# Inverse square roots of three LayerNorm steps: three Newton steps from a bit pattern, or ScalarE's square root and one Newton step

## The chip, the core and the metric

The kernel runs on one core of one Trainium2 chip. The metric is the device time of one execution in microseconds (us); smaller is better. TensorE is called PE, VectorE DVE, ScalarE ACT, GpSimdE POOL; SP is the engine that issues most DMAs.

## The reference

One layer of a hybrid decoder on 512 tokens of 1024 features, in float32:

```python
h = layer_norm(x, ln_in_g, ln_in_b)
mix = hybrid_mixer(h, ...)            # 16 state-space heads and 8 latent-attention heads
h = layer_norm(ALPHA * h + mix, ln_mix_g, ln_mix_b)
ffn = peer(h, ...)                    # 8 heads pick 16 of 16384 experts for each token
h = layer_norm(ALPHA * h + ffn, ln_ffn_g, ln_ffn_b)

def layer_norm(x, g, b):
    mu = mean(x);  var = mean((x - mu) ** 2)
    return (x - mu) * rsqrt(var + 1e-5) * g + b
```

Each LayerNorm needs, for each token, the inverse square root of a variance plus 1e-5. This study is about how that one number per token is found at two places: in the first LayerNorm, and in the last one for the third block of 128 tokens.

## The kernel before, in words

The 512 tokens are four blocks of 128, with tokens on the partitions. The kernel is one long function that issues the instructions of each engine in the order in which they stand in the text: nothing reorders them, and each engine works through its own queue. A wait on one engine therefore holds up all that is behind it on that engine.

Weights come through one stream, `win` (class `Stream`): SP loads an item of 128x1024 into a raw buffer `wir` (L91), ACT rounds it to the high part `wih` (L109, method `his`), DVE forms the low part `wil` as the difference (L119, method `splits`), and a raw buffer is loaded anew once `splits` has used it. A product in float32 is three matmuls: high by high (L72), low by high (L73), high by low (L74).

**The first LayerNorm (L260 to L296).** SP first issues the four loads of x into `XH` (L248), then constants and the first three weight items. The four blocks are treated as two halves, p = 0 and p = 1. For each half DVE takes the statistics of two blocks (L268, L269), adds 1e-5 (L272), and calls `rsqrt` (L130 to L139) on a tile of 128x2: a shift and a subtraction on the bit pattern give a first guess (L133, L134), and three Newton steps of three operations each refine it (L136 to L138). `nm` is minus the mean times that root (L274). Then the blocks are normalised in place: both of the first half on ACT (L279); of the second half one block and half of the other on DVE (L281) and the remaining 512 columns on ACT (L279). PE transposes each block in eight pieces into eight PSUM tiles (L284). After the first half's transposes the text calls `win.his(2)`, so ACT rounds two weight items ahead of its part of the second half.

Then, for each of eight pieces k, ACT applies the gain and the bias (`ht`, L291), ACT or DVE writes the rounded `HH` (L293, L295), DVE the low part `HL` (L296). Ahead of this loop stands the first `splits`, behind its first piece the second. PE starts the first two products of the input projection from these.

**The middle.** The input projection with the state-space part, attention, output projection, the second LayerNorm, the expert scores, and a long stage over the 128 groups of 128 experts. Tokens of the last block are handled by gathers and end early; the other three blocks end in the PSUM tiles `va`.

**The tail (L1470 to L1504).** `ln_out(b)` finishes blocks 0, 1 and 2 in this order on DVE: add the residual (L1480, or L1478 for block 2), statistics (L1482, L1484), the inverse root, two wide products per half row (L1499 or L1492, and L1501), and the output DMAs (L1502; SP issues them, and ACT the last). The inverse root comes from the generator `norm_chain` (L141 to L157): the same bit pattern guess (L147, L149) and three Newton steps of two operations each (L152, L154). For block 2 the two products that don't need the root (L1492) are set between its steps. ACT has one operation ahead of this part, the scaling of block 2's residual (L1504), and then nothing but the last output issue.

Of the kernel before, what the change touches and what calls it, by code (L numbers as in the profile page):

```python
# [11 lines left out]
F32 = mybir.dt.float32  # L12
# [5 lines left out]
AF = mybir.ActivationFunctionType  # L18
OP = mybir.AluOpType
# [7 lines left out]
EPS = 1e-5  # L27
# [26 lines left out]
def tile_block(ctx: ExitStack, tc: tile.TileContext, I, out):  # L54
# [74 lines left out]
    def rsqrt(p, v, shape, tag):  # L129
# [8 lines left out]
            V.scalar_tensor_tensor(y, b, 1.5, y, op0=OP.add, op1=OP.mult)  # L138
        return y  # L139

    def norm_chain(p, mv, tag, out):  # L141
        v = [p.tile([128, 1], F32, name=tag + n, bufs=2) for n in "vhay"]
        ve, hv, a, y = v
        V.tensor_scalar(ve, mv[:, 1:2], EPS, None, op0=OP.add)
        V.tensor_scalar(hv, mv[:, 1:2], EPS, -0.5, op0=OP.add, op1=OP.mult)
        yield
        V.tensor_scalar(a.bitcast(U32), ve.bitcast(U32), 1, None, op0=OP.logical_shift_right)  # L147
        yield
        V.tensor_scalar(y.bitcast(U32), a.bitcast(U32), -1.0, float(0x5F3759DF), op0=OP.mult, op1=OP.add)  # L149
        for _ in range(3):  # L150
            yield
            V.scalar_tensor_tensor(a, y, hv, y, op0=OP.mult, op1=OP.mult)  # L152
            yield
            V.scalar_tensor_tensor(y, a, 1.5, y, op0=OP.add, op1=OP.mult)  # L154
        out.append(y)
        yield
# [10 lines left out]
    def norm_stats(p, t, tag):  # L167
# [4 lines left out]
            pass  # L172
        return mv, o[0]

    cs2 = pool("cs2", side="right")
    C = cs2.tile([128, C_END], F32, name="C")
    PAR = cs2.tile([128, P_END], F32, name="PAR")
# [80 lines left out]
    nc.sync.dma_start(idb, I["cb"][:, 640:768])  # L258

    V.memset(ones, 1.0)  # L260
    mv4 = lnp.tile([128, NB, 2], F32, name="mv4")
    PS8 = [pa() if k < 4 else pb() for k in range(8)]
    for p in range(2):
        bs = slice(2 * p, 2 * p + 2)
        for b in (2 * p, 2 * p + 1):
            st6 = lnp.tile([128, 2, 6], F32, name="st6", bufs=2)
            for i in range(2):
                V.bn_stats(st6[:, i], XH[:, b, i * 512:(i + 1) * 512])  # L268
            V.bn_aggr(mv4[:, b], st6.rearrange("p a b -> p (a b)"))  # L269
        ve = lnp.tile([128, 2], F32, name="ve", bufs=2)  # L270
        nm = lnp.tile([128, 2], F32, name="nm", bufs=2)
        V.tensor_scalar(ve, mv4[:, bs, 1], EPS, None, op0=OP.add)  # L272
        rs = rsqrt(lnp, ve, [128, 2], "l0")
        V.scalar_tensor_tensor(nm, mv4[:, bs, 0], -1.0, rs, op0=OP.mult, op1=OP.mult)  # L274
        for j, cs, act in (((0, slice(0, D), 1), (1, slice(0, D), 1)) if p == 0 else
                           ((0, slice(0, D), 0), (1, slice(0, 512), 1), (1, slice(512, D), 0))):
            t = XH[:, 2 * p + j, cs]
            if act:
                A.activation(t, t, AF.Identity, bias=nm[:, j:j + 1], scale=rs[:, j:j + 1])  # L279
            else:  # L280
                V.tensor_scalar(t, t, rs[:, j:j + 1], nm[:, j:j + 1], op0=OP.mult, op1=OP.add)  # L281
        for k in range(8):
            for b in (2 * p, 2 * p + 1):
                T.transpose(PS8[k][:, b * 128:(b + 1) * 128], XH[:, b, k * 128:(k + 1) * 128], ident)  # L284
        if p == 0:
            win.his(2)
    win.splits(1)
    for k in range(8):
        ht = lnp.tile([128, S], F32, name="ht", bufs=3)
# [1141 lines left out]
    fin = None  # L1431
# [39 lines left out]
    def ln_out(b):  # L1471
        t = xr[b]
        st = fin.tile([128, 2, 6], F32, name="fst", bufs=2)
        mv = fin.tile([128, 2], F32, name="fmv", bufs=2)
        ce = [slice(e * 512, (e + 1) * 512) for e in range(2)]
        for e in range(2):
            if b == 2:
                V.scalar_tensor_tensor(t[:, ce[e]], va[b][e], scl, t[:, ce[e]], op0=OP.mult, op1=OP.add)  # L1478
            else:
                V.scalar_tensor_tensor(t[:, ce[e]], t[:, ce[e]], ALPHA, va[b][e], op0=OP.mult, op1=OP.add)  # L1480
            yield
            V.bn_stats(st[:, e], t[:, ce[e]])  # L1482
            yield
        V.bn_aggr(mv, st.rearrange("p a b -> p (a b)"))  # L1484
        yield
        o = []
        ch = norm_chain(fin, mv, "lf", o)
        for i, _ in enumerate(ch):
            yield
            if b == 2 and i in (2, 4):  # L1490
                cs = ce[i // 2 - 1]
                V.scalar_tensor_tensor(t[:, cs], t[:, cs], mv[:, 0:1], R2[:, 0, cs], op0=OP.subtract, op1=OP.mult)  # L1492
                yield
        rs = o[0]
        for e in range(2):
            cs = ce[e]
            if b < 2:
                yield
                V.scalar_tensor_tensor(t[:, cs], t[:, cs], mv[:, 0:1], R2[:, 0, cs], op0=OP.subtract, op1=OP.mult)  # L1499
            yield  # L1500
            V.scalar_tensor_tensor(t[:, cs], t[:, cs], rs, R2[:, 1, cs], op0=OP.mult, op1=OP.add)  # L1501
            (nc.scalar if b == 2 and e else nc.sync).dma_start(out[b * 128:(b + 1) * 128, cs], t[:, cs])  # L1502

    A.activation(xr[2], xr[2], AF.Copy, scale=ALPHA)  # L1504
    kept = sorted(held)
    for b, cc in ((0, kept[:4]), (1, kept[:2]), (0, kept[4:]), (1, kept[2:])):
        for c in cc:
# [91 lines left out]
```

## Time and profile before

| what | value |
| --- | --- |
| median of 3 runs | 1627.26 us (1627.14 to 1628.96) |
| the profiled execution, its own time | 1627.28 us |
| its span, first to last instruction | 1625.5 us |
| PE busy | 1582.6 us, 97% of the span |
| DVE busy | 1377.3 us, 85% |
| ACT busy | 699.8 us, 43% |
| DMA | 393.77 MB, mean 242 GB/s |

The profile is that of one execution. A row of its timeline reads: start in us, time taken in us, engine, line, operation, what is written and read, and in brackets how long the engine sat idle before and what released it. PEld is PE's loading of the stationary operand; SPq and ACTq are the issues of DMAs. The chain of work that ended last is followed back from the last instruction; a list of waits gives total, number and longest; a row of stretches gives busy time of each engine, with the clock that PE was granted behind them.

### The profile page before, as it was taken

How to read it: one execution, taken by the hardware profiler on the slowest of the kernel's cores; microseconds unless marked ns; L12 is line 12 of the kernel's file. 1: busy time of each engine (PE TensorE's matmuls, PEld its weight loads, DVE VectorE, ACT ScalarE, POOL GpSimd, SP SyncE). 2: the span in 40 equal slices, each digit the busy share in tenths (PEclk: the TensorE clock that was granted, in tenths of full speed). 3: DMA queues.
4: the chain of work that ended last, by engine and by line, in shares of the span. 5: the costliest groups of instructions: out<-in, count | busy, mean ns of one | idle time of the engine just before them, and what ended most of it. 6: DMA issues, size and time to landing. Idle time of an engine off the chain costs nothing.

```text
span 1625.5 us, 23770 instructions
## 1 busy us (share of the span) xinstructions
PE 1582.6 (97%) x8640; PEld 1394.3 (86%) x8640; DVE 1377.3 (85%) x2649; ACT 699.8 (43%) x1213; POOL 463.3 (29%) x332
## 2 busy tenths in 40 slices
PE   7999999999999999999899999999999999999997
PEld 5777878888888999998899999999999999888886
DVE  8979688947799999999588788788888888988977
ACT  5575466641433545555433333343333333333341
POOL 0000000000143213200155455555554544533300
PEclk9999999999999999999999999999999999999999
DMA  6242121374432458766799999999999999999973
GB/s 245 91 157 91 46 64 47 103 242 143 135 92 86 123 182 292 285 240 244 251 375 345 339 331 354 344 338 343 329 355 337 344 329 352 360 335 342 335 220 122
DMA packets 150604, 393.77 MB, mean 242 GB/s; under 512 B 12536, under 2 KB 64584, under 8 KB 148696
## 3 DMA queue, kind: packets, MB, share of 16 engines
q1 hardware_dynamic: 107400, 237.76, 43.3%
q0 software_dynamic: 42944, 154.24, 26.2%
q8 instruction: 67, 1.10, 0.3%
q14 instruction: 49, 0.40, 0.1%
q10 hardware_dynamic: 144, 0.26, 0.0%
HBM read 359.66 MB, written 31.51 MB: 241 GB/s over the span
## 4 chain that ended last, share of the span: by engine, by line
PE 74%; DVE 21%; ACT 2%; issue 2%; DMA 1%; DVEq 0%; ACTq 0%; SPq 0%
PE va L1352 10%; PE va L1356 10%; PE va L1353 10%; PE pu L72 8%; PE pu L74 8%; PE pu L73 8%; PE pa L74 3%; PE pa L73 3%; PE pa L72 3%; DVE wil L119 3%; DVE ij L1109 3%; DVE g L1113 2%; DVE t L953 1%; PE pw L73 1%; PE pw L74 1%
## 5 line engine op out<-in xcount | busy, mean ns | idle before, releaser
L109 ACT ACTIVATE wih<-wir 128x1024 fp32r<-128x1024 f32 (+2 forms) x269 | 277.9, 1034 | 264.5 <-DMA wir<-v 90.5
L119 DVE TENSOR_TENSOR wil<-wir,wih 128x1024 fp32r<-128x1024 f32 (+1 forms) x254 | 302.2, 1190 | 103.2 <-ACT wih L109 43.0
L74 PE MATMUL pu<-XTH,wil 128*128 128x368 f32 x1008 | 331.9, 329 | 0.7 <-DVE wil L119 0.7
L72 PE MATMUL pu<-XTH,wih 128*128 128x368 f32 x904 | 299.3, 331 | 0.0
L73 PE MATMUL pu<-XTL,wih 128*128 128x368 f32 x904 | 297.0, 329 | 0.0
L1353 PE MATMUL va<-wil,Ph 128*128 128x512 f32 x726 | 282.7, 389 | 0.0
L1389 POOL DMA_INDIRECT row<-u,ix x128 | 187.6, 1465 | 230.1 <-DVE row L1400 136.7
L1389 POOL DMA_INDIRECT row<-v,ix x128 | 181.3, 1416 | 196.0 <-DVE ac L1406 167.6
L74 PEld LDWEIGHTS pu<-XTH,wil 128*128 128x128 f32 x1008 | 189.3, 188 | 1.3 <-DVE wil L119 1.3
L73 PEld LDWEIGHTS pu<-XTL,wih 128*128 128x128 f32 x904 | 170.0, 188 | 2.9
L72 PEld LDWEIGHTS pu<-XTH,wih 128*128 128x128 f32 x904 | 169.8, 188 | 2.9
L1352 PE MATMUL va<-wih,Ph 128*128 128x512 f32 x432 | 168.5, 390 | 0.0
L1406 DVE SCALAR_TENSOR_TENSOR ac<-row,hd,ac 128x1024 f32<-128x1024 f32 x128 | 164.0, 1281 | 3.0 <-DMA row<-v,ix 0.9
L1353 PEld LDWEIGHTS va<-wil,Ph 128*128 128x128 f32 x726 | 136.3, 188 | 25.9
L1205 ACT ACTIVATE act<-pu 128x368 f32<-128x368 f32 x126 | 59.9, 476 | 221.3 <-PE pu L74 196.3
L1400 DVE SCALAR_TENSOR_TENSOR row<-row,x 128x1024 f32<-128x1024 f32 x128 | 150.1, 1219 | 2.4 <-DMA row<-u,ix 2.4
L109 ACT ACTIVATE wihx<-wir 128x1024 fp32r<-128x1024 f32 x67 | 71.1, 1061 | 158.3 <-DMA wir<-v 129.9
L1356 PE MATMUL va<-wih,Pl 128*128 128x512 f32 x432 | 133.4, 390 | 0.0
L119 DVE TENSOR_TENSOR wil<-wir,wihx 128x1024 fp32r<-128x1024 f32 x62 | 75.9, 1223 | 51.4 <-issue 45.5
L1352 PE MATMUL va<-wihx,Ph 128*128 128x512 f32 x294 | 114.9, 391 | 0.9 <-ACT Ph L1336 0.9
L1356 PEld LDWEIGHTS va<-wih,Pl 128*128 128x128 f32 x432 | 81.1, 188 | 17.2
L1352 PEld LDWEIGHTS va<-wih,Ph 128*128 128x128 f32 x432 | 81.2, 188 | 15.8
(458 smaller groups left out, 3073.7 us busy)
## 6 DMA issues: line engine op xcount, KB each, us to landing
wir<-ut SPq DMA_DIRECT2D x128, 512.0 KB
wir<-v SPq DMA_DIRECT2D x128, 512.0 KB
gsp<-stg SPq DMA_DIRECT2D x12, 1920.0 KB
gt<-gsp SPq DMA_DIRECT2D x30, 768.0 KB
wir<-wo SPq DMA_DIRECT2D x26, 512.0 KB
wir<-wf SPq DMA_DIRECT2D x18, 512.0 KB
wir<-wqr SPq DMA_DIRECT2D x16, 512.0 KB
de<-acd POOLq DMA_DIRECT2D x8, 512.0 KB
```

The source lines that it names most:

```text
L72: T.matmul(ps, lh, rh, start=start, stop=False)
L73: T.matmul(ps, lh, rl, start=False, stop=False)
L74: T.matmul(ps, ll, rh, start=False, stop=stop)
L109: A.activation(h, r, AF.Copy)
L119: self.lo(n).tensor_tensor(l, r, h, op=OP.subtract)
L1205: A.activation(ACT[c][:, :NU], ps, AF.Gelu)
L1352: T.matmul(va[b][e], Ph[:, bs], h[:, cs], start=c == 0, stop=False)
L1353: T.matmul(va[b][e], Ph[:, bs], l[:, cs], start=False, stop=False)
L1356: T.matmul(va[b][e], Pl[:, bs], h[:, cs], start=False, stop=c == 127)
L1389: G.indirect_dma_start(out=R[s], out_offset=None, in_=I["u"] if s < 128 else I["v"], in_offset=bass.IndirectOffsetOnAxis(ap=ix[:, s % 128: ...
L1400: V.scalar_tensor_tensor(r, r, 1.0, x3, op0=OP.mult, op1=OP.mult, accum_out=hd[:, s:s + 1])
L1406: V.scalar_tensor_tensor(ac, r, hd[:, s - 128:s - 127], ac, op0=OP.mult, op1=OP.add)
```

## The change

A new function `sqrt_rs` takes the place of `rsqrt` in both halves of the first LayerNorm: ACT takes the square root of the variance with 1e-5 as its bias operand, while DVE forms -0.5 times the sum; then DVE takes the reciprocal and does one Newton step in three operations. The separate addition of 1e-5 (L272) is gone. A generator `sqrt_chain` does the same for block 2 of the tail, with a Newton step of two operations, and the two wide products now stand behind its first and its second step. A tile `eps` holds the constant. Two operations on a scrap tile `w0` take a square root on ACT ahead of need, one at the very start and one behind the scaling of block 2's residual. Last, one of the two weight roundings that ACT did behind the first half now stands ahead of ACT's part of the second half, behind the second square root, and the other behind that part.

```diff
+    def sqrt_rs(p, v, shape, tag):
+        h, q, y, a = (p.tile(shape, F32, name=tag + n) for n in "hqya")
+        A.activation(q, v, AF.Sqrt, bias=eps)
+        V.tensor_scalar(h, v, EPS, -0.5, op0=OP.add, op1=OP.mult)
+        V.reciprocal(y, q)
+        V.tensor_tensor(a, y, y, op=OP.mult)
+        V.tensor_tensor(a, a, h, op=OP.mult)
+        V.scalar_tensor_tensor(y, a, 1.5, y, op0=OP.add, op1=OP.mult)
+        return y
+
+    def sqrt_chain(p, mv, tag, out):
+        h, q, a, y = (p.tile([128, 1], F32, name=tag + n) for n in "hqay")
+        A.activation(q, mv[:, 1:2], AF.Sqrt, bias=eps)
+        V.tensor_scalar(h, mv[:, 1:2], EPS, -0.5, op0=OP.add, op1=OP.mult)
+        yield
+        V.reciprocal(y, q)
+        yield
+        V.scalar_tensor_tensor(a, y, h, y, op0=OP.mult, op1=OP.mult)
+        yield
+        V.scalar_tensor_tensor(y, a, 1.5, y, op0=OP.add, op1=OP.mult)
+        out.append(y)
+        yield
...
     V.memset(ones, 1.0)
+    V.memset(eps, EPS)
     mv4 = lnp.tile([128, NB, 2], F32, name="mv4")
+    w0 = lnp.tile([128, 1], F32, name="w0")
+    A.activation(w0, ones[:, 0:1], AF.Sqrt, bias=eps)
...
-        ve = lnp.tile([128, 2], F32, name="ve", bufs=2)
         nm = lnp.tile([128, 2], F32, name="nm", bufs=2)
-        V.tensor_scalar(ve, mv4[:, bs, 1], EPS, None, op0=OP.add)
-        rs = rsqrt(lnp, ve, [128, 2], "l0")
+        rs = sqrt_rs(lnp, mv4[:, bs, 1], [128, 2], f"l{p}")
         V.scalar_tensor_tensor(nm, mv4[:, bs, 0], -1.0, rs, op0=OP.mult, op1=OP.mult)
+        if p:
+            win.his(1)
...
-        if p == 0:
-            win.his(2)
+    win.his(2)
     win.splits(1)
...
-        ch = norm_chain(fin, mv, "lf", o)
+        ch = (sqrt_chain if b == 2 else norm_chain)(fin, mv, "ls" if b == 2 else "lf", o)
         for i, _ in enumerate(ch):
             yield
-            if b == 2 and i in (2, 4):
-                cs = ce[i // 2 - 1]
+            if b == 2 and i in (0, 1):
+                cs = ce[i]
...
     A.activation(xr[2], xr[2], AF.Copy, scale=ALPHA)
+    w0 = fin.tile([128, 1], F32, name="w0")
+    A.activation(w0, xr[2][:, 0:1], AF.Square)
+    A.activation(w0, w0, AF.Sqrt, bias=eps)
```

More of the change, by code (lines that the diff above doesn't have):

```diff
@@ L173, in norm_stats @@
         return mv, o[0]
+    ep = pool("ep", side="right")
+    eps = ep.tile([128, 1], F32, name="eps")
     cs2 = pool("cs2", side="right")
```

## The prediction

> **What bounds the kernel now.** I read the page first: who owns the chain that ended last, and what TensorE (PE) waited for.
>
> ```profile
> PE 74%; DVE 21%; ACT 2%; issue 2%; DMA 1%; DVEq 0%; ACTq 0%; SPq 0%
> ```
> ```profile
> PE pa L284 <- ACT XH L279: 11.6, 2, 10.9
> ```
>
> The first line is the chain by engine: PE owns 74% of the span, VectorE (DVE) 21%. The second opens the list of PE's waits (total, times, longest, in us): its longest, 10.9 us, is the wait for the first normalised block, at the very start. No wait of that list names a transfer. So whatever advances PE's start should be carried through the middle, where each stage is released by the one before it, and whatever is cut behind the last matmul is saved outright. The change works at these two ends, so I read the timeline of each.
>
> ```profile
> 6.81 0.21 DVE L269 BATCH_NORM_AGGREGATE mv<-st 128x2 f32<-128x12 f32 x1
> 7.05 0.17 DVE L272 TENSOR_SCALAR ve<-mv 128x2 f32<-128x2 f32 x1
> ...
> 7.87 0.33 SPq L254 DMA_DIRECT2D HR<-hrow  x1
> ...
> 9.21 0.33 SPq L91 DMA_DIRECT2D wir<-wf  x1
> ...
> 9.42 0.16 DVE L274 SCALAR_TENSOR_TENSOR nm<-mv,l0y 128x2 f32<-128x2 f32 x1
> ...
> 9.62 2.37 ACT L279 ACTIVATE XH<-XH,nm,l0y 128x1024 f32<-128x1024 f32 x2 [4.19 <-DVE nm L274]
> ...
> 10.89 0.33 SPq L258 DMA_DIRECT2D idb<-cb  x1
> ...
> 11.89 1.99 ACT L109 ACTIVATE wih<-wir 128x1024 fp32r<-128x1024 f32 x2
> ...
> 12.20 0.21 DVE L269 BATCH_NORM_AGGREGATE mv<-st 128x2 f32<-128x12 f32 x1
> ...
> 13.38 1.72 PEld L284 LDWEIGHTS pb<-ident,XH 128*128 128x128 f32 x8
> ...
> 14.82 0.16 DVE L274 SCALAR_TENSOR_TENSOR nm<-mv,l0y 128x2 f32<-128x2 f32 x1
> 15.02 0.81 ACT L279 ACTIVATE XH<-XH,nm,l0y 128x512 f32<-128x512 f32 x1 [1.14 <-DVE nm L274]
> ...
> 15.88 0.86 PEld L284 LDWEIGHTS pa<-ident,XH 128*128 128x128 f32 x8 [0.79 <-DVE XH L281]
> ...
> 16.20 1.22 DVE L119 TENSOR_TENSOR wil<-wir,wih 128x1024 fp32r<-128x1024 f32 x1
> 16.36 1.45 ACT L291 ACTIVATE ht<-pa,PAR 128x512 f32<-128x512 f32 x2 [0.54 <-PE pa L284]
> ...
> 17.34 0.42 DVE L295 CAST HH<-ht 128x512 fp32r<-128x512 f32 x1
> ...
> 20.27 0.19 PEld L73 LDWEIGHTS pa<-HL,wih 128*128 128x128 f32 x1 [0.30 <-DVE HL L296]
> ```
>
> From the aggregate (6.81) to nm (9.42) DVE walks twelve tiny dependent operations, about 0.195 us apart after a first step of 0.24, while ScalarE (ACT) idles 4.19 us. The same walk, 12.20 to 14.82, delays the second half. After 20.27 PE has no wait left in this stage: that is the moment I follow.
>
> **The change, step by step.** New is a 128x2 square root on ACT with a bias operand. The nearest groups (mean ns of one behind the comma):
>
> ```profile
> L456 ACT ACTIVATE de<-de,nac 128x128 f32<-128x128 f32 x64 | 19.6, 390 | 2.7 <-DVE de L461 2.7
> ...
> L279 ACT ACT_TABLE_LOAD x1 | 1.3, 1283 | 4.1 <-DMA XH<-x 4.1
> ...
> L1402 ACT ACTIVATE hd<-hd 128x128 f32<-128x128 f32 x1 | 0.3, 310 | 2.9 <-DVE row L1400 2.9
> ...
> L1057 ACT ACTIVATE uhd<-uhd 128x16 f32<-128x16 f32 x1 | 0.2, 218 | 0.0
> ```
>
> A 128x128 with a bias operand takes 0.39, without one 0.31; a 128x16 without one 0.22. I take 0.22 + 0.08 = 0.30, between bounds of 0.22 and 0.39. ACT followed nm by 0.20 (9.42 to 9.62), as a dependent DVE step would, so I give the way over the 0.24 and the way back 0.03. The reciprocal I price as any small DVE step.
>
> *First half.* Aggregate 6.81, square root 7.05 to 7.35, reciprocal 7.38, then four steps of 0.195 to nm: 8.16 in place of 9.42, **1.26 earlier**. DVE's half product (L144 of the changed kernel) runs beside the square root. The first table load (1.28) waits for x today; it moves ahead of that wait, with a warm-up root on a constant, under the time in which x is still loading: nothing. The 128x1 memset hides there too. DVE now reaches the third and fourth block of x 1.26 earlier, near 8.24 and 9.7. SP's HR issue (7.87) and third weight issue (9.21) waited, by the profile, for just these landings, so the data is there, by 0.4 us or more.
>
> *Second half.* Aggregate 12.20 - 1.26 = 10.94. ACT is done with the first two blocks at 9.62 + 2.37 - 1.26 = 10.73, so the second root isn't delayed; nm comes at 10.94 + 1.35 = 12.29 in place of 14.82, **2.53 earlier**. Of the two weight roundings that ACT did before this half (11.89, two in 1.99) only one now stands between, 11.5 to 12.5, and its weights had landed by 10.89, when idb's issue stopped waiting for them; it may end 0.01 or so after ACT would start normalising at 12.49. The other follows, 13.3 to 14.3.
>
> *PE's transposes.* The first half's last eight take 1.72 (0.215 each) from 13.38 and end at 15.10; moved by 1.26, at 13.84. The second half, which waited for XH until 15.88, is ready by then (12.49 + 0.81) and starts at 13.84, 2.0 earlier. In the run before it ran twice as fast (eight in 0.86): PE's pace doubled between 15.10 and 15.88. If it doubles at the same clock time, some eight go slowly and eight fast, to 13.84 + 1.72 + 0.86 = 16.4.
>
> *ht, HH, HL and the weights' low parts.* ht followed the transposes by 0.48; at the slow pace 0.2 more, so 14.5. HH follows 0.8 later at 15.3 in place of 17.34, where it waited for wil's end (16.20 + 1.22 = 17.42); that end is now 2.53 earlier and no longer last. HL, second wil and the 20.27 mark follow HH: 2.0 earlier. PE needs seven matmuls first, 0.23 each: 16.4 + 1.6 = 18.0, in time for 18.3. If the slow pace lasted through all 16 transposes, PE would arrive at 18.9, 1.4 earlier. If it rose early, wil binds: 2.5. I take **1.9**, range 1.2 to 2.5. Weight loads are issued when wil frees their buffers and move forward with it.
>
> *The middle.* In the changed program PE's and SP's orders are as before, and DVE's and ACT's differ only at the two ends; I cost it at nothing and carry 1.9 through.
>
> *The tail.* The last block:
>
> ```profile
> 1596.12 1.04 ACT L1504 ACTIVATE xr<-xr 128x1024 f32<-128x1024 f32 x1
> ```
> ```profile
> 1617.68 0.15 DVE L144 TENSOR_SCALAR lfv<-fmv 128x1 f32<-128x1 f32 x1
> ...
> 1618.06 0.15 DVE L149 TENSOR_SCALAR lfy<-lfa 128x1 uint32<-128x1 uint32 x1
> 1618.13 0.74 DVE L1492 SCALAR_TENSOR_TENSOR xr<-xr,fmv,R 128x512 f32<-128x512 f32 x1
> 1618.79 0.21 DVE L152 SCALAR_TENSOR_TENSOR lfa<-lfy,lfh 128x1 f32<-128x1 f32 x1
> 1619.03 0.16 DVE L154 SCALAR_TENSOR_TENSOR lfy<-lfa,lfy 128x1 f32<-128x1 f32 x1
> ...
> 1620.47 0.16 DVE L154 SCALAR_TENSOR_TENSOR lfy<-lfa,lfy 128x1 f32<-128x1 f32 x1
> 1620.66 1.41 DVE L1501 SCALAR_TENSOR_TENSOR xr<-xr,lfy,R 128x512 f32<-128x512 f32 x2
> 1622.16 0.37 ACTq L1502 DMA_DIRECT2D out_dram<-xr  x1
> ```
>
> New order: h at 1617.68; first wide product 0.07 later (as 1618.06 to 1618.13), 1617.75; reciprocal 0.66 on, 1618.41; second wide product 0.07 on, 1618.48; a 0.66 on, 1619.14; y 0.24 on, 1619.38; L1501 0.19 on, 1619.57 in place of 1620.66: **1.09 earlier**. ACT's root runs 1617.69 to 1618.0, covered by the first wide product with 0.4 to spare; uncovered it would cost at most its 0.3. Its table load is the only one added to the program: behind L1504 (ends 1597.2), before ACT's next work at 1622.16, so 1.28 in some 20 us of idleness. The output issue stays behind the root on ACT's queue; the root is done 3 us earlier.
>
> *Sum.* Profiled execution: span 1625.5, time 1627.28, 1.8 around it, 0.02 above the median 1627.26. 1627.28 - 1.9 - 1.09 = **1624.3**.
>
> **The rivals.** PE's clock by stretches (columns: length, busy PE, PEld, DVE, ACT, POOL, then the granted clock), and the chain behind:
>
> ```profile
> 222.13:225.54 3.41, 1.90 (x13) 1.34 (x11) 2.84 (x9) 2.00 (x6) 0.00 (x0) 1.00 0.00 0
> 223.64:227.05 3.41, 1.35 (x5) 0.63 (x4) 2.83 (x9) 3.23 (x9) 0.00 (x0) 1.00 0.00 0
> ...
> 227.05:230.46 3.41, 3.41 (x10) 2.64 (x9) 2.83 (x6) 0.48 (x1) 0.00 (x0) 0.50 0.33 96
> 261.19:264.60 3.41, 2.00 (x13) 1.37 (x11) 3.30 (x10) 2.37 (x6) 0.00 (x0) 1.00 0.43 124
> 264.60:268.01 3.41, 2.29 (x14) 1.76 (x14) 3.10 (x11) 2.23 (x6) 0.00 (x0) 1.00 0.02 5
> ```
> ```profile
> 227.24 0.43 PE pu L72
> ...
> 230.63 0.23 PE pu L74
> ```
>
> A stretch in which PE was busy 1.35 of 3.41 us is followed by one at half clock, in which eight matmuls of the chain take 0.43, not 0.23: 1.6 us. A stretch with 2.00 busy (261.19) is not followed by one.
>
> *(a) The half-clock stretch goes.* If the 3.41 us marks stand at the same times after the start, work that comes 1.9 earlier puts into the stretch before 223.64 what now lies in 222.13 to 225.54: 1.90 busy, nearer to the harmless 2.00 than to 1.35. Then 1.6 us more are saved: **1622.7**. For it: 227.05 - 62 x 3.41 = 15.6, between the 15.10 and 15.88 where PE's pace doubled, so one row of marks holds through the run. Against: the limit is unseen between 1.35 and 2.00.
>
> The Trainium skill, "TensorE: Matmul & The Clock Gate", section "What's actually happening", says the window of about 3.4 us is free-running and isn't reset by a kernel's start, so that the point of change varies from run to run. The trace's 3.41 us stretch agrees; no single trace shows the rest. By that rule (a) would come and go between runs of either kernel, instead of following from the shift.
>
> *(b) The crossings are dear.* If each way between DVE and ACT cost 0.3 more than I gave, the two roots of the start would lose 1.2, the tail 0.2 (0.6 less its 0.4 of cover): **1625.7**. A late first weight, which now stands ahead of ACT's part of the second half, would act alike. Against: 9.42 to 9.62. This is also the case in which the change hardly does what it says.
>
> *(c) Slower: new half-clock stretches.* The shift may as well push another stretch below the limit; 261.19 (2.00) and its neighbour (2.29) have the next idle spots. Each costs 1.6: one gives 1625.9, two **1627.5**, above 1627.28; from two on it is slower than before, from four on by over 0.2%.
>
> **How the numbers follow.** Forecast 1624.3: 0.42 (own range 1623.6 to 1625.1). (a) 0.32. (b) 0.12. (c) one stretch 0.09, two or more 0.05. The range runs from (a) with a gain 0.7 above my sum, 1622.0, to (c) with one stretch and 0.4 of loss, 1626.3. A measurement of this kernel can tell about 0.2% from no change, 3.25 us, so faster means below 1624.0: all of (a) and three tenths of the forecast, 0.45; slower (above 1630.5) 0.03; the rest 0.52.
>
> **What would show it.** nm at 8.2 and 12.3; second transposes from 13.8; PE without waits from 18.4; L1501 1.1 earlier behind lfv's place; one table load more, between 1597 and 1617; a half-clock stretch near 225 or none. I am wrong if XH's normalisation waits for a transfer, if the reciprocals wait over 0.1 behind the root's end, or if PE's lead of 1.9 is gone by 30 us.

## The result, and the profile after

The changed kernel takes **1633.11 us** (median of 7 runs, 1632.91 to 1634.32) against 1627.84 us for the kernel before on the same chip (7 runs, 1627.14 to 1630.21): a ratio of 1.0032, 95% interval 1.0022 to 1.0042. It is slower. The forecast was 1624.3, with 1622.0 to 1626.3 as its range. The profiled execution took 1632.91 us, 5.63 more than the profiled one before; its span is 1631.2 us.

Both edits do what they are for. The head, in the timeline of the changed kernel (start, time taken, engine, line):

```profile
6.84 0.21 DVE L297 BATCH_NORM_AGGREGATE mv<-st 128x2 f32<-128x12 f32 x1
7.09 0.30 ACT L143 ACTIVATE l0q<-mv,eps 128x2 f32<-128x2 f32 x1 [4.75 <-DVE mv L297]
...
7.42 0.17 DVE L145 RECIPROCAL l0y<-l0q 128x2 f32<-128x2 f32 x1 [0.16 <-ACT l0q L143]
...
8.20 0.16 DVE L300 SCALAR_TENSOR_TENSOR nm<-mv,l0y 128x2 f32<-128x2 f32 x1
...
8.40 2.37 ACT L307 ACTIVATE XH<-XH,nm,l0y 128x1024 f32<-128x1024 f32 x2 [1.01 <-DVE nm L300]
...
12.34 0.16 DVE L300 SCALAR_TENSOR_TENSOR nm<-mv,l1y 128x2 f32<-128x2 f32 x1
...
13.87 1.72 PEld L312 LDWEIGHTS pa<-ident,XH 128*128 128x128 f32 x8
...
14.75 1.45 ACT L318 ACTIVATE ht<-pa,PAR 128x512 f32<-128x512 f32 x2 [0.45 <-PE pa L312]
...
18.51 0.19 PEld L73 LDWEIGHTS pa<-HL,wih 128*128 128x128 f32 x1 [0.30 <-DVE HL L323]
```

`nm` comes at 8.20 and 12.34 instead of 9.42 and 14.82, and the mark that stood at 20.27 now stands at 18.51: 1.76 earlier. The tail, in the same view:

```profile
1603.39 1.28 ACT L1534 ACT_TABLE_LOAD   x1
```
```profile
1624.27 0.21 DVE L1511 BATCH_NORM_AGGREGATE fmv<-fst 128x2 f32<-128x12 f32 x1
1624.51 0.15 DVE L154 TENSOR_SCALAR lsh<-fmv 128x1 f32<-128x1 f32 x1
1624.51 0.29 ACT L153 ACTIVATE lsq<-fmv,eps 128x1 f32<-128x1 f32 x1 [19.54 <-DVE fmv L1511]
...
1626.40 1.42 DVE L1528 SCALAR_TENSOR_TENSOR xr<-xr,lsy,R 128x512 f32<-128x512 f32 x2
```

From the first operation behind the aggregate to the last wide products it is 1.89 (1624.51 to 1626.40) where it was 2.98 (1617.68 to 1620.66). That is 1.09 saved, as forecast. Yet all of this block lies 5.74 us later than before (1626.40 against 1620.66). The time was lost in between, where the text of the program is the same.

Where? Take PE's matmuls in order of time and compare the start of the one with the same number in the two traces; both have 8640. The table gives the start after minus the start before, worked out from the two traces, at some of those matmuls (their time before in the first line):

```
time before (us)      80     216    304    403    542    758    841    1398   1584
after - before (us)  -1.86  -1.75  -1.64  -1.32  +1.45  +1.43  +1.92  +6.47  +6.47
step                        +0.11  +0.10  +0.33  +2.77  -0.02  +0.49  +4.55   0.00
```

Most of the lead of the head is there until 304 us. (The 0.49 belongs to a stretch at half clock near 784 us, which lasts 6.83 us instead of 3.41.) Two steps destroy it: 2.77 from 403 to 542, 4.55 from 841 to 1398. A last 0.36 is lost between 1584 us and the aggregate, in the same way: the last 72 matmuls that take `XTH` or `XTL` as their moving operand (at the end these tiles hold weight items) start, on average of each group, 5.7 to 7.5 ns further apart, PE's last matmul is another 0.59 later, and DVE passes on 0.36 of it. Is PE waiting in the two long steps? The stretches of the two kernels (length, busy PE with its instructions, PEld, DVE, ACT, POOL, granted clock), before and then after:

```profile
403.00:542.00 139.00, 137.99 (x723) 120.45 (x722) 128.60 (x788) 51.11 (x77) 47.12 (x20) 1.00 0.34 105
841.00:1398.00 557.00, 557.00 (x2883) 506.37 (x2882) 464.04 (x594) 208.34 (x345) 288.11 (x199) 1.00 0.96 341
```
```profile
403.00:542.00 139.00, 137.99 (x709) 118.36 (x708) 128.16 (x795) 49.97 (x75) 45.83 (x20) 1.00 0.34 102
841.00:1398.00 557.00, 557.00 (x2865) 506.19 (x2864) 459.02 (x590) 207.18 (x344) 289.74 (x198) 1.00 0.95 338
```

No: PE is as busy as before, at full clock, in both. It only gets through fewer matmuls: 709 instead of 723 in the first stretch, 14 x 139 / 723 = 2.7 us. The matmuls follow one another a little more slowly. The groups by form say which ones. From 400 to 545 us, before and after (mean ns of one behind the comma):

```profile
L74 PE MATMUL pw<-XTH,wil 128*128 128x512 f32 x128 | 49.9, 390 | 0.0
L72 PE MATMUL pw<-XTH,wih 128*128 128x512 f32 x96 | 38.4, 400 | 0.2 <-ACT XTH L914 0.2
L73 PE MATMUL pw<-XTL,wih 128*128 128x512 f32 x96 | 37.5, 391 | 0.2 <-DVE XTL L915 0.2
```
```profile
L74 PE MATMUL pw<-XTH,wil 128*128 128x512 f32 x128 | 50.6, 395 | 0.0
L72 PE MATMUL pw<-XTH,wih 128*128 128x512 f32 x96 | 39.0, 406 | 0.2 <-ACT XTH L941 0.2
L73 PE MATMUL pw<-XTL,wih 128*128 128x512 f32 x96 | 38.1, 397 | 0.2 <-DVE XTL L942 0.2
```

and on the whole page, before and after:

```profile
L72 PE MATMUL pu<-XTH,wih 128*128 128x368 f32 x904 | 299.3, 331 | 0.0
...
L1353 PE MATMUL va<-wil,Ph 128*128 128x512 f32 x726 | 282.7, 389 | 0.0
```
```profile
L72 PE MATMUL pu<-XTH,wih 128*128 128x368 f32 x904 | 302.7, 335 | 0.0
...
L1380 PE MATMUL va<-wil,Ph 128*128 128x512 f32 x726 | 283.3, 390 | 0.0
```

The groups shown that read `XTH` or `XTL` (the transposed, split input of the expert stage) take 4 to 6 ns longer; `va<-wil,Ph`, 512 columns wide too, goes from 389 to 390. Matmuls overlap, so the time from start to start counts: for 512 columns 227 ns before and 233 after (means of L74), for L72's 368 columns 168 and 171 (medians). From 841 to 1398 us the 1632 matmuls that read the streams account for 3.51 of the 4.55. The other 1.03 lies in the `va` matmuls, which read neither stream: they come in blocks of 18 behind the stream's, and of each block only the first nine change, on average by 1.7 ns.

The program has one difference that touches these tiles. The constant `eps` got a pool of its own, `ep`, as the first of the right side of the on-chip memory, which is filled from the top down. (The diff ahead of the prediction doesn't show the two lines that do this; they stand under b32 below.) Its 4 bytes per partition take 32, and **every later tile of that side starts 32 bytes lower**: XTH at 196448 instead of 196480, XTL at 212832 instead of 212864 (bytes within the partition, from the built programs). The weights `wih` and `wil` lie on the left side and did not move (28800 for the first).

### The profile page after: what moved, and what is told of

Its sections match the earlier page's. It is cut to its first block, busy times and chain, and to the rows that moved or that the text cites. A ratio compares the mean times of both kernels' runs of the same rounds, so it can differ in the third digit from the quotient of the medians.

```text
span 1631.2 us, 23757 instructions
## 1 busy us (share of the span) xinstructions
PE 1593.9 (98%) x8640; PEld 1402.7 (86%) x8640; DVE 1372.8 (84%) x2630; ACT 703.8 (43%) x1220; POOL 471.6 (29%) x332
## 4 chain that ended last, share of the span: by engine, by line
PE 89%; DVE 8%; ACT 2%; issue 1%; DMA 0%; DVEq 0%; ACTq 0%
PE pu L72 11%; PE pu L74 10%; PE va L1380 10%; PE va L1379 10%; PE va L1383 10%; PE pu L73 10%; PE pw L73 3%; PE pw L74 3%; PE pw L72 3%; PE pa L72 3%; PE pa L74 3%; PE pa L73 3%; DVE ij L1136 2%; DVE wil L119 1%; DVE g L1140 1%; PE pb L519 1%
## 5 line engine op out<-in xcount | busy, mean ns | idle before, releaser
L74 PE MATMUL pu<-XTH,wil 128*128 128x368 f32 x1008 | 334.3, 332 | 0.0
L72 PE MATMUL pu<-XTH,wih 128*128 128x368 f32 x904 | 302.7, 335 | 0.0
L1416 POOL DMA_INDIRECT row<-u,ix x128 | 191.9, 1499 | 228.9 <-DVE row L1427 136.5
L1416 POOL DMA_INDIRECT row<-v,ix x128 | 185.5, 1450 | 193.8 <-DVE ac L1433 165.3
L74 PEld LDWEIGHTS pu<-XTH,wil 128*128 128x128 f32 x1008 | 189.8, 188 | 0.0
L72 PEld LDWEIGHTS pu<-XTH,wih 128*128 128x128 f32 x904 | 170.5, 189 | 2.9
```

The source lines that it names most:

```text
L72: T.matmul(ps, lh, rh, start=start, stop=False)
L74: T.matmul(ps, ll, rh, start=False, stop=stop)
L1416: G.indirect_dma_start(out=R[s], out_offset=None, in_=I["u"] if s < 128 else I["v"], in_offset=bass.IndirectOffsetOnAxis(ap=ix[:, s % 128: ...
```

## The experiments

My theory was that the streams' new start alone costs the 7.3 us, through the pace of PE. The rivals were the new work itself (a longer ACT and DVE program, an earlier start that meets other transfers) and the half-clock stretches. Starts are given against the kernel before. The steps 403 to 542 and 841 to 1398 are those of the table above, always against the profiled execution before.

### 1. The pool without the roots, the roots with other pads

**b32**: the kernel before, with nothing but the pool, the tile and its memset.

```diff
+    ep = pool("ep", side="right")
+    eps = ep.tile([128, 1], F32, name="eps")
...
+    V.memset(eps, EPS)
```

> The kernel before with nothing of the change but the 4-byte tile on top of the right side and its memset; roots, order and tail are as before. Theory A: it loses what the changed kernel lost in the middle, 8.2 us, without the gains: 1636, from 1635 to 1637. Theory B: 1627.8, as before. Theory C: as A.

Measured: 1635.77 against 1629.05, ratio 1.0042 (1.0028 to 1.0055); steps 2.77 and 4.55, to the hundredth those of the changed kernel. No root was touched. The loss is that of the tile.

**xt32**: the kernel before, XTH and XTL 32 lower, the tiles allocated behind them 64 lower, and nothing ahead of them moved.

```diff
+    xt.tile([128, 1], F32, name="xpad")
+    xq = pool("xq", side="right")
+    xq.tile([128, 1], F32, name="qpad")
```

> The kernel before with 32 bytes of padding in the pool of XTH and XTL and 32 more below it, so that these two alone start 32 bytes off a multiple of 64; all tiles allocated after them lie 64 bytes lower, those before them where they were. Theory A with XTH and XTL as the cause: the matmuls that read them lose 7.7 us, 1635.5, from 1634.7 to 1636.3. If instead other tiles of the right side are to blame (those of the attention, the gather's rows, the key tables): 1627.8 to 1628.5.

Measured: 1635.44, ratio 1.0040 (1.0026 to 1.0053); steps 2.66 and 4.54. In both steps the delays lie where they do in the changed kernel, in the matmuls that read the two tiles and the `va` ones behind them. So these two tiles suffice. What remained was the rule.

**p64** and **p96**: the changed kernel with a wider constant (16 or 24 numbers), which puts the streams 64 and 96 lower. For p64:

```diff
-    eps = ep.tile([128, 1], F32, name="eps")
+    eps = ep.tile([128, 16], F32, name="eps")[:, 0:1]
```

> The changed kernel with the constant's tile made 64 bytes wide instead of 4 (which the allocator rounds to 32), so that every tile of the right side starts on a multiple of 64 bytes again, as before the change. Theory A (PE streams the moving operands XTH and XTL slower when they start 32 bytes off a multiple of 64): the matmuls on them start every 227 ns (512 columns) again and not 233, the drift after 400 us is gone, and the two saved stretches remain: 1627.8 - 1.8 - 1.1 = 1624.9, from 1624.3 to 1625.8. Theory B (the new work on ACT and DVE slows the middle, by whatever way): 1633, as the changed kernel. Theory C (it is how far the tiles lie from the top, not the remainder): 1633 or more, as the shift is doubled.

> The changed kernel with the constant's tile 96 bytes wide: XTH starts 32 bytes off a multiple of 64 once more, 96 bytes below its old place. Theory A: 1633.1, from 1632.6 to 1633.8, as with 32 bytes. Theory B: 1633 too. Theory C: the loss grows with the distance, 8.3 us for 32 bytes, so well above 1636.

Measured: p64 1633.25, ratio 1.0026 (1.0017 to 1.0036), steps 2.58 and 5.00; p96 1629.41, ratio 1.0004 (0.9994 to 1.0013), steps 2.84 and 0.45. My first rule, that a start must be a multiple of 64, **fell** with p64; all three theories missed p96, where the 512-wide matmuls lost and the 368-wide ones hardly did.

### 2. Streams higher, and the changed kernel with the streams back

**xtup32**, **xtup64**, **xtup96**: the kernel before, with small tiles that lay above the streams moved below them (`scl`, `one`, or both), so that the streams lie 32, 64 and 96 higher and nothing else moves. The first of them:

```diff
-    scl = xt.tile([128, 1], F32, name="scl")
+    xq = pool("xq", side="right")
+    scl = xq.tile([128, 1], F32, name="scl")
```

> The kernel before with scl alone (32 bytes) moved below XTH and XTL, which so start 32 HIGHER (196512): the same remainder to 128 as 96 lower, where the 512-wide matmuls lost and the 368-wide did not. Theory (the remainder to 128 decides): 512-wide 233 to 234 ns, 368-wide unchanged at 168, 2.2 to 3.3 slower in all, ratio 1.0017 (1.0010 to 1.0024). Rival (lower starts lose, higher ones don't): 1.0000. Rival (a shift by 32 either way loses alike): 6.4 slower, ratio 1.0040.

> The kernel before with the tile one (64 bytes) alone moved below XTH and XTL, which so start 64 HIGHER (196544): the same remainder to 128 as 64 lower, where the 512-wide matmuls went 227 to 233 and the 368-wide 168 to 170. All else as before. Theory (the remainder to 128 decides): both again, 5 to 7 slower, ratio 1.0037 (1.0028 to 1.0046). Rival (a start is good where it is a multiple of 64, and the loss 64 lower came from elsewhere): 1.0000.

> The kernel before with the tiles one and scl (96 bytes) moved below XTH and XTL, which so start 96 HIGHER (196576): the same remainder to 128 as 32 lower, which the changed kernel has. All else as before. Theory (the remainder of the start to 128 decides): 6.4 slower, ratio 1.0040 (1.0030 to 1.0048), 512-wide matmuls on the streams 233 ns and 368-wide 171 from start to start. Rival (the direction or the distance to other tiles decides, lower starts lose): as before, 1.0000 (0.9992 to 1.0008). Rival (any other place than the tuned one loses by its distance): more than 6.4.

Measured: xtup32 ratio 1.0023 (1.0014 to 1.0032), steps 2.45 and 1.82; xtup64 1.0021 (1.0011 to 1.0030), steps 0.86 and 1.83; xtup96 1.0045 (1.0030 to 1.0060), steps 2.95 and 1.81. With b32, p64 and p96 six shifted starts have lost time in the first step, lower and higher ones, so it isn't that lower is bad. But the remainder to 128, my second rule, fails on the size: 96 higher has the same remainder as 32 lower and costs 1.81 instead of 4.54 in the second step; 64 higher costs 0.86 in the first where 64 lower costs 2.58. (xtup96's ratio holds a further 1.41 between 542 and 758 us, where p96 and xtup32 gained 1.56 and 1.00; I didn't find out why.)

**aup32**: the changed kernel as it is, with the edit of xtup32: `scl`'s 32 bytes go below the streams, which so start at 196480 again. Its roots, its pool and the places of all other right-side tiles are the changed kernel's.

> The changed kernel with its constant in its own pool as it stands, and the 32-byte tile scl moved from the pool of XTH and XTL to a pool of its own below them. The two streams start at 196480 again; every other tile of the right side stays where the changed kernel has it (32 lower). Theory (only the start of XTH and XTL matters): as the kernel with the constant elsewhere, 2.7 to 3.0 less than before, ratio 0.9982. Rival (the other tiles of the right side, moved by 32, take a part): between 0.9990 and 1.0032.

Measured: **1626.18** (1624.42 to 1627.08, 11 runs) against 1628.74, ratio **0.9984** (0.9975 to 0.9993); steps 0.12 and 0.00. With one small tile moved, the change that was 0.32% slower is faster than the kernel before.

**loc**: the changed kernel with the constant where it moves no tile, for the head in `lnp`, for the tail in `fin`.

```diff
-    ep = pool("ep", side="right")
-    eps = ep.tile([128, 1], F32, name="eps")
...
+    eps = lnp.tile([128, 1], F32, name="eps")
     V.memset(eps, EPS)
...
                 xr = [fin.tile([128, D], F32, name=f"xr{b}") for b in range(3)]
+                eps2 = fin.tile([128, 1], F32, name="eps2")
+                V.memset(eps2, EPS)
```

> The changed kernel, all of it, with the constant held where it moves no other tile: a tile in the first LayerNorm's own pool for the first two roots, and a second one, written by VectorE, allocated last in the pool of the last block for the final root. XTH starts at 196480 again, as in the kernel before. Theory (the start of XTH and XTL alone took the middle's time): the head's 1.6 to 1.9 and the tail's 1.09 both reach the end, 2.7 to 3.0 less than before, ratio 0.9982 (0.9978 to 0.9988); `pw<-XTH,wih` back at 227 ns from start to start and `pu<-XTH,wih` at 168. Rival (the middle's time comes from the roots' new instructions or from when the streams start): ratio 1.0025 or more, as in the changed kernel. Rival (the head's gain is lost to waits in the middle in any case, the tail's stays): 1.1 less, ratio 0.9993.

Measured: 1627.41, ratio 0.9996 (0.9987 to 1.0005): 1.2 us short of aup32. Its head stayed 1.72 to 1.80 ahead up to 758 us, but at 1591 us PE lost 1.4. The waits of DVE and then of ACT in loc from 1575 to 1600 us (total, times, longest) show my own mistake:

```profile
DVE eps L1486 <- DMA out_dram<-ac: 4.0, 1, 4.0
```
```profile
ACT XTL L109 <- DMA wir<-v: 4.7, 1, 4.7
```

The second constant took over memory from which a transfer was still reading, so its memset stood 4.0 us on DVE's queue; DVE's next split came late, SP's next load behind it, and ACT waited 4.7 us for weights, where the kernel before waits 3.2. **loc2** writes that constant after all loads are issued.

```diff
-                eps2 = fin.tile([128, 1], F32, name="eps2")
-                V.memset(eps2, EPS)
...
+    eps2 = fin.tile([128, 1], F32, name="eps2")
+    V.memset(eps2, EPS)
     w0 = fin.tile([128, 1], F32, name="w0")
```

> The changed kernel with the constant held where it moves no tile, as in the first run of that kind, but the last root's constant written right ahead of the last sums, so that its write no longer waits for the transfer out of the tile that lay there before (that write held VectorE for 4.0 us and the last weights came late, 1.45 at 1591 us). Theory: the head's 1.75 and the tail's 1.09 together, 2.8 less than before, ratio 0.9983 (0.9978 to 0.9988). Rival (the head's gain is given back at the half-clock stretches or at a transfer): 1.1 less, 0.9993.

Measured: 1626.03 (1624.43 to 1628.14) against 1627.62, ratio 0.9988 (0.9979 to 0.9997); no stall at 1591. The 2.8 expected lies just inside the interval; its profiled execution, 1624.86, led by about 1.5 until 758 us, 0.3 less than expected; I didn't find out why.

### 3. Each half alone

With the streams kept at 196480 by the edit of xtup32: **h32**, only the head's change; **t32**, only the tail's; **ctl32**, only the pool, tile and memset of b32.

> The changed kernel's first half alone (the two roots of the first LayerNorm, the moved roundings, the constant), the last block's norm as before, and scl moved below the streams so that XTH and XTL start at 196480. Theory (the head's gain reaches the end once the streams keep their start): 1.3 to 1.9 less than before, ratio 0.9990 (0.9987 to 0.9993). Rival (the middle swallows what the head gains, at waits for transfers or at the clock): 1.0000, and the change's only gain is the tail's.

> The changed kernel's other half alone: the last norm's root by ScalarE and one Newton step, the head as before, the constant in its own pool and scl moved below the streams so that XTH and XTL start at 196480. Theory (the tail's 1.09 is free of everything ahead of it): 1.09 less than before, ratio 0.9993 (0.9990 to 0.9997). Rival (the table's load for the root, now late on ScalarE, delays a store or an earlier block's norm): 1.0000 or above.

> The kernel before with the constant's pool and its memset, as in the run that had only these and was slower by 1.0042, but with scl moved below the streams, so that XTH and XTL start at 196480; the right side's other tiles stay 32 lower. No root is changed. Theory (nothing but the streams' start counts): 1.0000 (0.9992 to 1.0008). Rival (the other tiles' places or the memset take a part): 1.0010 to 1.0042.

Measured: h32 0.9996 (0.9987 to 1.0005), t32 0.9999 (0.9990 to 1.0008), ctl32 1.0005 (0.9996 to 1.0015). All three are 0.8 to 1 us worse than I expected, and the two halves can't be told from no change one by one. The traces say why: from 216 to 542 us each of them, and aup32 too, loses 0.5 to 0.6 (ctl32 0.59 in steps of 0.09, 0.35 and 0.15), which loc and loc2, where no tile of the right side moved, don't (0.05 and 0.02). Some 0.4 of ctl32's 0.59 lies in the output projection. Its weight items 10 to 13 are kept in a pool of their own on the right side (`hold`, L888), 32 lower too, and are streamed against `MH` and `ML`, which lie on the left and didn't move. Each product there is the triple of L72 to L74. With these four items a triple takes 11 to 17 ns more, all but the first of each block of tokens; with items 8 and 9, which aren't kept, it takes the same time as before. The rest is in small pieces that I leave open. From 380 to 410 us, one group in which both kinds are mixed, before and in ctl32:

```profile
L73 PE MATMUL pw<-wil,MH 128*128 128x512 f32 x24 | 9.3, 389 | 0.0
```
```profile
L73 PE MATMUL pw<-wil,MH 128*128 128x512 f32 x24 | 9.4, 393 | 0.0
```

(In xt32 and p64 the kept items lie 64 lower, and there the kernel gains 0.35 and 0.33 from 304 to 403 us: in the kernel before, their place wasn't the best one.) With this 0.6 the sums fit: head -1.8 + 0.6 = -1.2 (measured 0.0004 x 1628 = -0.7), tail -1.1 + 0.6 = -0.5 (-0.2), both -2.2 (aup32: -2.6), none +0.6 (+0.8); each is within its interval of 1.5 us.

### 4. The pace by itself

**swap**: XTL allocated ahead of XTH, so that they change places; both starts stay what they were as a pair.

```diff
-    XTH = xt.tile([128, 8, S], F32R, name="XTH")
     XTL = xt.tile([128, 8, S], F32R, name="XTL")
+    XTH = xt.tile([128, 8, S], F32R, name="XTH")
```

> The kernel before with XTL allocated ahead of XTH: the two change places (XTH at 212864, XTL at 196480), both still multiples of 128, everything else where it was. Theory (an aligned start is enough): 1.0000 (0.9992 to 1.0008), paces 227 and 168. Rival (the tuned place of each stream, or which is lower): 1.0015 to 1.0045, as in the six shifted starts.

Measured: 0.9998 (0.9989 to 1.0007), steps 0.02 and 0.00. It isn't one tuned place.

**map** and **mapc** are kernels of matmuls alone, the triples of L72 to L74 over eight slices:

```python
def block(name, i, n, groups):      # streams start 32 * i bytes into XT
    ...
    for g in range(groups):
        for k in range(8):
            mm3(ts[g % 2][:, :n], wih[:, k], wil[:, k], h[:, k, :n], l[:, k, :n], k == 0, k == 7)
```

> A kernel that computes nothing of the reference: only rows of matmuls of the form that the middle runs (wih with XTH, wih with XTL, wil with XTH, eight slices to a sum), first 512 and then 368 columns wide, 120 to a row, with the streams' start 128, 96, 64, 32 lower than 196480, at it, and 32, 64, 96 higher (rows a to h), there and back; the weights stay at 28800. No other engine works. Theory (alignment of the start to 128 by itself): rows a and e 227 and 168 ns from start to start, the others 231 to 237, and up to 171 or 173. Rival (the tuned place only): row e alone is fast. Rival (it takes other engines' accesses beside it): all rows alike, 227 and 168.

> The same rows of matmuls, with VectorE (subtractions of 1024 columns) and ScalarE (copies of 1024 columns) at work all the time on tiles that have nothing to do with them. Theory (alignment by itself): the same pace as without them. Rival (contention with other engines' accesses): flat without them, and here 6 ns more in the rows that aren't aligned.

Measured: the effect is there without any other engine, and the same beside VectorE and ScalarE (at 32 lower 234.2 ns from start to start in both), although the two were busy for 97% of the time, so contention with them is out. But 128 lower, a multiple of 128 too, was slow: 233.2 and 234.1. That refutes the rule of 128, and since 196352 and 196480 differ from the weights' 28800 by 654.5 and 655 times 256, it left two readings: the streams' own place with a period of 256, or their distance to the weights. **mapw** moves the weights too.

> Rows of matmuls alone again (nothing of the reference is computed), 120 of 512 columns and 120 of 368 to a row. Rows x: the streams' start 128 lower to 96 higher than 196480 in steps of 32, weights at 28800. Rows w: the weights moved so, streams at 196480. Rows b: both moved by the same amount. Rows f: the streams 512, 448, 384, 320, 256, 224, 192, 160 lower, weights at 28800. Theory D (the distance between streams and weights decides, with a period of 256): w as slow as x where the weights are moved by other than 0, b all at 227 to 228 ns, f fast at 512 and 256 lower alone. Theory S (the streams' own place, period 256): x and b alike, w all at 227 to 228, f fast at 512 and 256 lower. Theory T (both places, each by itself): w slow, b slow.

Measured, as mean ns from start to start over the 119 steps of a row, 512 columns (and 368):

```
moved by (bytes)   -128         -96          -64          -32          0            +32          +64          +96
x  streams alone   234.1 (174.2) 235.1 (167.6) 234.2 (169.8) 234.2 (169.8) 227.8 (167.6) 234.2 (168.7) 229.9 (167.6) 234.2 (174.2)
w  weights alone   234.2 (174.2) 234.2 (169.8) 234.2 (167.6) 234.2 (168.7) 227.9 (167.6) 234.1 (169.8) 234.2 (169.8) 235.2 (167.5)
b  both            227.8 (167.6) in all eight
f  streams alone   -512: 227.8 (167.6)   -256: 227.6 (167.6)   -448: 230.0   -192: 229.9   the other four: 233.3 to 234.2
```

Moving both leaves the pace as it is, and moving the weights up is as moving the streams down: in 368 columns +32 of the weights has the 169.8 of -32 of the streams, -32 has the 168.7 of +32, -64 the 167.6 of +64. So the **distance** decides whether a row of 512 columns is at the fast pace, and with a period of 256 bytes (rows b and f). How slow the others are it doesn't settle alone: 64 gives 229.9 where the streams go up and 234.2 where the weights go down. (96 gives 174.2 and 169.8 so in 368 columns, but there one and the same place took both paces in map, 174.0 on the way there and 169.8 back.) One view of it, the extent of four groups in mapw (first and last start in us; wxe nothing moved, wxd streams 32 lower, wwd weights 32 lower, wbd both):

```profile
L72 PE MATMUL wxe<-XT,W x40: 389/389/501, 253.5 to 280.2; 128*128 128x512 f32 x40
```
```profile
L72 PE MATMUL wxd<-XT,W x40: 395/396/503, 204.6 to 232.0; 128*128 128x512 f32 x40
```
```profile
L72 PE MATMUL wwd<-XT,W x40: 393/396/497, 594.7 to 622.1; 128*128 128x512 f32 x40
```
```profile
L72 PE MATMUL wbd<-XT,W x40: 389/389/497, 981.7 to 1008.3; 128*128 128x512 f32 x40
```

The same 40 matmuls of L72 span 26.7, 27.4, 27.4 and 26.6 us. Now the kernel's steps can be worked out: 128 + 96 + 96 + 32 + 32 = 384 matmuls of 512 columns read the streams between 400 and 545 us, at 6.4 ns each 2.5 us (2.45 to 2.95 measured for five of the six shifts), at 64 higher 2.1 ns each, 0.8 us (0.86 measured). For 368 columns the rows don't give the step. They give, within 1.3 us, what the 1632 matmuls on the streams take of it, and tell the dear places (32 and 64 lower, 96 higher) from the cheap ones. The rest is in the first nine `va` matmuls of the blocks behind (from the tenth on 0.00):

```
streams moved by (bytes)                 -32    -64    -96    +32    +64    +96
step from 841 to 1398 us                +4.55  +5.00  +0.45  +1.82  +1.83  +1.81
of it in the matmuls on the streams     +3.51  +3.73  +0.74  +0.51  +0.40  +3.80
by the rows, 1632 x the difference      +3.6   +3.6    0.0   +1.8    0.0   +3.6 (169.8) or +10.8 (174.2)
of it in the va matmuls behind          +1.03  +1.26  -0.28  +1.31  +1.43  -1.99
```

The `va` matmuls take 0.00 more where the streams keep their distance to the weights (aup32, swap, both32), so the streams' place causes this too; how it reaches matmuls that don't read them isn't shown.

**both32** puts the answer to the test in the whole kernel: streams 32 higher as in xtup32, and the left side, with the weights, 32 higher too.

```diff
+    lp = pool("lp")
+    lp.tile([128, 1], F32, name="lpad")
     wst = pool("wst")
...
-    scl = xt.tile([128, 1], F32, name="scl")
+    xq = pool("xq", side="right")
+    scl = xq.tile([128, 1], F32, name="scl")
```

> The kernel before with XTH and XTL 32 higher (scl moved below them, as in the run that was slower by 1.0023) and, with a 32-byte tile ahead of the weights' pool, all tiles of the left side 32 higher too, the weights among them (28832). Theory D (the distance of streams and weights to a multiple of 256): the 512-wide step from 403 to 542 us 0.0 to 0.5 instead of 2.45, the 368-wide one from 841 to 1398 us 0.0 instead of 1.82; what may stay is the 0.6 that the other right-side tiles cost from 216 to 542 us when they alone lay 32 apart from the left; ratio 1.0004 (0.9996 to 1.0012). Theory S (the streams' own place): as with the streams alone, 1.0023.

Measured: 1628.47 against 1627.45, ratio 1.0003 (0.9994 to 1.0013); steps 0.11 and 0.00, where xtup32 had 2.45 and 1.82. The same groups in xtup32 and then in both32, from 400 to 545 us:

```profile
L74 PE MATMUL pw<-XTH,wil 128*128 128x512 f32 x128 | 50.5, 395 | 0.0
L72 PE MATMUL pw<-XTH,wih 128*128 128x512 f32 x96 | 39.0, 406 | 0.2 <-ACT XTH L915 0.2
```
```profile
L74 PE MATMUL pw<-XTH,wil 128*128 128x512 f32 x128 | 49.9, 390 | 0.0
L72 PE MATMUL pw<-XTH,wih 128*128 128x512 f32 x96 | 38.4, 400 | 0.2 <-ACT XTH L917 0.2
```

In the whole kernel, too, it is the distance.

## Why the prediction was wrong, step by step

- **First half**: 1.26 forecast; nm at 8.20 instead of 9.42, 1.22. The root took 0.30, as estimated, and the way back 0.03 (7.39 to 7.42). Right.
- **Second half**: 2.53 forecast, 2.48 measured (14.82 to 12.34). Its share of x was there in time; the weight rounding ahead of ACT's part ended at 12.47, within 0.07 of where ACT went on (12.54). Right.
- **PE's transposes** from 13.84: 13.87 measured. **The mark at 20.27**: 1.9 forecast, 1.76 measured, because ht came at 14.75 instead of 14.5. Right within its range of 1.2 to 2.5.
- **The tail**: 1.09 forecast, 1.09 measured; the table load ran at 1603.39, hidden as said.
- **The middle**: "In the changed program PE's and SP's orders are as before, and DVE's and ACT's differ only at the two ends; I cost it at nothing and carry 1.9 through." This step failed. The orders were as before, but the addresses weren't. Of the three lines that make `eps` (pool, tile, memset) I costed the memset and not the place that the tile takes. In its place the runs show 2.77 + 4.55 = 7.3 us (b32 and xt32 have it without the roots, aup32 has the roots without it): PE gets through the matmuls on XTH and XTL, and the `va` ones right behind them, more slowly. Another 0.36 is lost so at the end, and some 0.4 from 216 to 403 us, for the most part at the kept weight items (ctl32). No wait shows it, and the prediction had looked at waits alone: no entry of PE's list of waits is longer than before. All signs that it named held, down to the lead of 1.9 (1.86 at 80 us); none of them looked at the middle.
- **The sum**: -1.86 (the lead at 80 us) + 0.11 + 0.10 + 0.33 + 2.77 - 0.02 + 0.49 + 4.55, then 0.36 from 1584 us to the aggregate, then -1.09: 5.74, the shift of the last wide products; 1632.91 - 1627.28 = 5.63.
- **Rival (a)**: the half-clock stretch near 227 didn't go in the profiled execution. Its rows in the changed kernel (columns as in the prediction):

```profile
220.94:224.35 3.41, 1.37 (x12) 0.90 (x10) 2.84 (x8) 2.57 (x7) 0.00 (x0) 1.00 0.00 0
224.35:227.76 3.41, 3.41 (x6) 2.09 (x7) 3.30 (x9) 0.77 (x3) 0.00 (x0) 0.50 0.31 96
```

  The stretch ahead again has only 1.37 us of busy PE: the marks moved with the run. In aup32, b32, swap and both32 the stretch ahead of the half clock holds 1.57, 1.53, 1.54 and 1.71 us of busy PE, so the limit lies above 1.71; whether it lies below (a)'s 1.90 stays open. In the profiled executions of the experiments it stands at 224 (aup32), near 227 (xtup96), at 266 (swap), or nowhere (xt32). By the Trainium skill ("TensorE: Matmul & The Clock Gate", "What's actually happening"), the window runs free of the kernel's start; these runs agree: b32 and swap begin as the kernel before does, and have the stretch at 266 instead of 227.
- **Rival (b)**: not so, the crossings were at the price given. **Rival (c)**, the only one on the slower side, had the wrong mechanism (a longer half-clock stretch took 0.49 of the loss), and with 0.03 for slower nearly all chance of this outcome was missing. With the streams where they were, the kernel comes into the forecast's range: by the ratios, 1627.28 x 0.9988 = 1625.3 (loc2, no tile of the right side moved) and 1627.28 x 0.9984 = 1624.7 (aup32), each within 1.5 either way. Loc, with its own mistake, is at 1626.6, above the range.

## What to carry to other kernels

When a diff adds a tile, however small, work out the start of every later tile of that side, and count it as a change to all matmuls that read them and to those right behind. Here the distance between the streamed operand and the weights had been a multiple of 256 bytes, and 32 bytes on it cost 6.4 of 228 ns for each 512-wide matmul. If PE is equally busy in a stage, at full clock, and gets through fewer matmuls, compare groups of the same form and look at addresses before looking for waits; and put a new constant where it moves nothing, or pad the side back.

## What the runs showed of the hardware

- TensorE's pace on streams of 512 float32 columns depends on the distance of the stream's start to that of the weights, modulo 256 bytes: 227.8 ns from start to start at 0, 229.9 with the stream 64 higher, 233.2 to 235.2 at the other multiples of 32 (and 234.2 with the weights 64 lower); for 368 columns 166.5 to 174.2, with 167.6 at 0. It does so with no other engine at work. Why isn't shown; that the load of the next weights (188 ns, beside the running matmul) and the stream meet in the same part of the memory is an argument only. The Trainium skill, "TensorE: Matmul & The Clock Gate", "Step-by-step: what each phase is for", says that streaming and weight loading read through two ports of their own, and that loading the next tile's weights takes no bandwidth from the running matmul. By that, moving the weights alone (rows w of mapw) shouldn't change the pace; it goes from 227.9 to 234.1 and up to 235.2, and the measurement decides.
- The same row of 368 columns can settle at two paces: 128 lower took 166.5 on the way there and 174.2 on the way back in map, and 96 higher 174.0 and 169.8. Which one it takes I can't say.
